# A hybrid decoder layer on one core: the first projection fed by k tiles, some waits re-ordered, and two early transfers issued by ScalarE

## The chip, the cores and the metric

The kernel runs on one core of a Trainium2 chip. The metric is the device time of one execution in microseconds (us). A core has five instruction streams that matter here: TensorE (PE in the profile; PEld are its weight loads), VectorE (DVE), ScalarE (ACT), GpSimd (POOL) and SyncE (SP), which only issues transfers. ACT can issue transfers too; ACTq and SPq are the rows for that.

## The reference

One layer over x of 256 tokens by 2048 channels, all in float32:

```python
h = rmsnorm(x, norm_mix_pre)
xr, yr, q, k, v, g_rnn, g_attn = split(h @ w_in)
y_rnn = rg_lru(conv(xr)) * gelu(yr)
y_att = sliding_window_sink_attention(rope(q), rope(k), v, sinks)   # 32 query heads, 4 key/value heads of 64
mix = sigmoid(g_rnn) * (y_rnn @ w_rnn_proj) + sigmoid(g_attn) * (y_att @ w_attn_proj)
x = x + rmsnorm(mix @ w_out, norm_mix_post)
u = square(relu(rmsnorm(x, norm_mlp_pre) @ w_mlp_up))               # 8192 wide
x = x + rmsnorm(u @ w_mlp_down, norm_mlp_post)
```

## The kernel before, in words

**Products.** Each float32 operand is split into a rounded part "hi" and a remainder "lo"; a product is three matmuls, hi·hi, hi·lo and lo·hi. `Stream` (L56 to L170) feeds the weights: a half chunk of 128 x 1024 floats (512 KB) is loaded into `wraw`, ACT casts it into `whi` (L107, L116), DVE subtracts to get `wlo` (L108, L124). There are four `wraw` buffers and six each of `whi` and `wlo`; `ahead` (L151) keeps the split six halves in front of PE.

**The opening (L342 to L470).** k and v of all 256 tokens are one product over 16 k tiles of 128 channels, accumulated in two banks `kv`, one for each block of 128 tokens. The weights `w_kv` come as eight halves of two k tiles each; x transposed (`x_t`) comes as five further transfers; the gains lie in the table `tiny`, which ACT loads (L350) while SP issues all else. `part(k)` (L400) multiplies a tile of x by its gain on ACT and makes the remainder on DVE: `hT`. `split_first` (L66) splits the first half in two pieces, `kv_step` (L408) issues the matmuls (L415), 12 for each half and pass over tokens; ten matmuls on a tile of ones (`warm`, L396) run in front. Loads of the next weights (`w_g`) and of x itself (`xq`, for the norm) follow on SP.

**The passes that follow.** Gates and queries (`b_pass512`), then the recurrent branch (`a_pair`, L256). Attention is a generator for each of four head groups; `pump` advances the oldest generator by one step at four places in each `a_pair` and at one in each step of `b_pass512`, so its instructions lie between the matmuls of the projection. `turn_probs` (L625) transposes the probabilities on PE into banks `pt`, which ACT copies out (L638).

**The norm between mix and MLP (L950 to L1040).** The last matmuls of `w_out`, the norm of the second token block (`norm(1)`), its transposes (`turned`, L973, into two banks used in turn) and the first matmuls of the MLP (`up_step`, L1027) are interlaced by hand. `high` (L978, ACT) and `low` (L983, DVE) empty a bank.

**The end (L1142 to L1285).** `down` sums 16 pairs of k tiles into four output blocks (token block, column block); seven of the pairs are combined in seven products in place of eight (`SEVEN`, the last is pair 12), and their sums are added into tiles `ready` (L1175 to L1179) and to the running sum `acc` (L1243). Pair 13 goes to all four blocks, then for each block in turn come the matmuls of pairs 14 and 15 and `finish` (L1260): add the bank (L1269), square with a running sum on ACT (L1270), multiply by the gain (L1271); after a token block's last column block follow sum, square root, reciprocal (L1275 to L1277), the scaled addition (L1283) and the store (L1284).

**Order.** Each engine runs its instructions in order. What `pin` wraps keeps the order of the program; the rest is ordered by the framework's planner, which gives earlier lines priority among those that are ready by its own reckoning.

Of the kernel before, what the change touches and what calls it, by code (L numbers as in the profile page):

```python
# [53 lines left out]
class Stream:  # L54
# [3 lines left out]
    def __init__(self, nc, pool, chunks, room, sums):  # L58
        self.nc, self.pool, self.chunks, self.room, self.sums = nc, pool, chunks, room, sums
        self.raw, self.parts = {}, {}  # L60
        self.loaded = self.split = 0
        self.pin = lambda i: i
        self.high = []
        self.at = 0

    def split_first(self, between):  # L66

        src = self.raw.pop(0)
        hi = self.pool.tile([P, 1024], F32R, tag="whi", bufs=WHALF, name="whi0")
        lo = self.pool.tile([P, 1024], F32R, tag="wlo", bufs=WHALF, name="wlo0")  # L70
        for i in range(2):
            c = slice(i * 512, i * 512 + 512)
            self.pin(self.nc.scalar.copy(hi[:, c], src[:, c]))
            between(i)
            self.pin(self.nc.vector.tensor_tensor(lo[:, c], src[:, c], hi[:, c].bitcast(F32), ALU.subtract))
        self.parts[0] = hi, lo
        self.split = 1

    def load_to(self, n):
        while self.loaded < min(n, 2 * len(self.chunks)):  # L80
            j = self.loaded
            c = slice(j % 2 * 1024, j % 2 * 1024 + 1024)
            if j < 2 * EXTRA:
                if j % 2 == 0:
                    self.place = self.room(f"wraw{j}")
                t = self.place[:, c]
            else:
                t = self.pool.tile([P, 1024], F32, tag="wraw", bufs=WRAW, name=f"wraw{j}")
            self.latest = self.nc.sync.dma_start(t, self.chunks[j // 2][:, c])
            self.raw[j] = t  # L90
            self.loaded += 1
# [85 lines left out]
EXTRA = 5  # L177


def layer(tc, x, x_t, few, pos_row, gains, w_kv, w_q, w_xy, w_rg, w_g, w_rp, w_ap, w_out,  # L180
# [13 lines left out]
    chunks = [w_kv[i] for i in range(4)]  # L194
# [145 lines left out]
    xts = [flat(unit(f"xt{i}", F32)) for i in range(2)]  # L340

    def xt(k, n=1):  # L342
        return xts[k // 8][:, k % 8 * S : (k % 8 + n) * S]

# [4 lines left out]
    tiny = const.tile([P, 210], F32, name="tiny")  # L349
    nc.scalar.dma_start(tiny, few)  # L350
    gcol, ifr, sink = [tiny[:, a : a + n] for a, n in ((0, KT), (16, 32), (48, NH))]
    vec = tiny[:, 80:208].rearrange("p (a b) -> p a b", a=8)
    pos_i = tiny[:, 208:210].bitcast(I32)

    def load_xt(a, b):
        q, c = a // 4, slice(a % 4 * S, a % 4 * S + (b - a) * S)
        nc.sync.dma_start(xt(a, b - a), x_t[q][:, c])
# [13 lines left out]
    ws.load_to(2 * EXTRA + WRAW)  # L371
# [6 lines left out]
    sq = const.tile([P, 4, TB, 4], F32, name="sqs")  # L378
# [21 lines left out]
    def part(k):  # L400
        q, i, g, src = k // 4, k % 4, gcol[:, k : k + 1], xt(k)
# [6 lines left out]
    def kv_step(j):  # L408
        hi, lo = ws.half(False)
        for ks in ((0,), (1,)) if j == 0 else ((0, 1),):  # L410
            for x, w in ((0, hi), (1, hi), (0, lo)):
                for tb in range(TB):
                    for i in ks:
                        kt = 2 * j + i
                        pin(mm(kv[tb], hT[kt // 4][:, kt % 4, x, tb * P : tb * P + P], w[:, quarter(i)],  # L415
                               start=kt == 0 and w is hi and x == 0, stop=kt == KT - 1 and w is lo))
# [40 lines left out]
    ws.split_first(part)  # L457
    kv_step(0)
    angle = angles()
    for j in range(1, 8):  # L460
        for i in range(2):
            part(2 * j + i)
        ws.split_high()
        ws.split_low()
        kv_step(j)
        if j > 3:
# [84 lines left out]
    def attention(g, banks):  # L551
# [73 lines left out]
        def turn_probs(tb, pars=(0, 1)):  # L625
# [5 lines left out]
            for par in pars:  # L631
                for kb in range(nk):
                    ps = bank(psm, "pt")
# [37 lines left out]
        yield  # L671
        turn_probs(1, (1,))
        yield
        for tb in range(TB):
# [280 lines left out]
    def norm(tb, between=None, late=None):  # L955
# [4 lines left out]
        if between:  # L960
            between()
        pin(nc.vector.reciprocal(a, b))
        for q in range(4):
            c = quarter(q)
            if q == 3 and late:
                late()
            pin(nc.vector.scalar_tensor_tensor(h2[tb][:, c], h2[tb][:, c], a, xg[tb][:, c], ALU.mult, ALU.add))
        r1.append(a)

# [47 lines left out]
    norm(1, lambda: low(0, 3), lambda: gained(1, 3, banks[1][1]))  # L1017
    for j in range(3):
# [12 lines left out]
    for q, n in enumerate((26, 6, 6, 6)):  # L1031
# [4 lines left out]
        high(1, q)  # L1036
        low(1, q)
        if q == 1:
# [92 lines left out]
    def product(b, a, w, begun, tail=False):  # L1131

        for i, (x, y) in enumerate(((0, 0), (0, 1), (1, 0))):
            mm(b, a[x], w[y], start=not begun and i == 0, stop=tail and i == 2)  # L1134
# [7 lines left out]
    def down(f, n, uT, held, order, finish, early, between=lambda p: None, behind=lambda: None):  # L1142
# [8 lines left out]
        def step(p, parts, names):  # L1151
            for name in names:
                at, n2 = name
                b = PLACE[name]
                for i, (hi, lo) in enumerate(parts):
                    t = slice(at * P, at * P + P)
                    c = quarter(n2)
                    a = uT[p][:, i]
                    product(banks[b], (a[:, 0, t], a[:, 1, t]), (hi[:, c], lo[:, c]), b in begun,
                            p == PAIRS - 1 and i == 1)  # L1160
                    begun.add(b)

        ready = {}
        for p in range(PAIRS - held):
            if p in SEVEN:
                parts = ws.seven()
                for name, (i, w) in LEFT.items():
                    product(banks[name], (uT[p][:, 0, i], uT[p][:, 1, i]), parts[w], name in begun,
                            p == SEVEN[-1] and name in ("P1", "P6", "Q5", "N7"))
# [11 lines left out]
            else:  # L1181
                for i in range(2):
                    hi, lo = ws.half()
                    for name in order:
                        at, n2 = name
                        b = PLACE[name]
                        t, c = slice(at * P, at * P + P), quarter(n2)
                        a = uT[p][:, i]
                        product(banks[b], (a[:, 0, t], a[:, 1, t]), (hi[:, c], lo[:, c]), b in begun)
                        begun.add(b)  # L1190
            between(p)
        parts = [[ws.half(False) for i in range(2)] for p in range(held)]
        behind()
        for name in order:
            for i in range(held):
                step(PAIRS - held + i, parts[i], (name,))
            finish(name, banks[PLACE[name]], ready[name])
        ws.ahead(ws.at - 1)

    for f in range(2):  # L1200
# [25 lines left out]
        if f == 0:  # L1226
            for n in range(2):
                def finish(name, b, t):
# [31 lines left out]
        def finish(name, b, t):  # L1260
# [4 lines left out]
            if n == 0:  # L1265
                nc.vector.tensor_tensor(a, b, t, ALU.add)
                nc.scalar.activation(t, a, AF.Square, accum_out=sq[:, 3, tb, q : q + 1])
                return
            pin(nc.vector.tensor_tensor(a, b, t, ALU.add))  # L1269
            pin(nc.scalar.activation(spare[:, c], a, AF.Square, accum_out=sq[:, 3, tb, q : q + 1]))  # L1270
# [100 lines left out]
```

## Time and profile before

| | us |
|---|---|
| median of 3 runs (1502.19 to 1502.8) | 1502.19 |
| the profiled execution's own time | 1502.42 |
| its span, first to last instruction | 1500.6 |
| PE busy | 1485.3 |
| DVE busy | 1097.8 |
| ACT busy | 829.6 |

The profile is one execution taken by the hardware profiler. The span is 1.8 us shorter than the execution's time; the rest lies around it. A busy PE says that matmuls were in flight, not that they ran at full clock, so the granted clock is read beside it. A row of the timeline gives start, duration, engine, line of the code, operation, what is written and read, shapes, and in brackets how long the engine had idled before and what released it.

### The profile page before, as it was taken

To read this page: it belongs to the slowest core of one execution; us is meant where nothing else is said; L and a number is where in the kernel's file an instruction comes from. 1 tells how busy PE (TensorE), PEld (TensorE's weight loads), DVE (VectorE), ACT (ScalarE), POOL (GpSimd) and SP (SyncE) were. 2 spreads that over 40 slices of the span, in tenths; PEclk is the share of its full clock that TensorE was granted. 3 is DMA by queue.
4 is the path that set the end of the run, shared out by engine and by line. 5 is a ranking of instruction groups with operands and counts; after the bars stand their busy time and mean duration, and the time that the engine had idled before them with its cause. 6 is when DMAs were issued, how large, how long until landed. Compare 5 with 4: busy or idle time off the path is not lost.

```text
span 1500.6 us, 19926 instructions
## 1 busy us (share of the span) xinstructions
PE 1485.3 (99%) x7568; PEld 1259.0 (84%) x7568; DVE 1097.8 (73%) x1356; ACT 829.6 (55%) x1137; POOL 1.7 (0%) x9
## 2 busy tenths in 40 slices
PE   9999999999999999999999999999999999999997
PEld 7887788788889888888889888888888888888886
DVE  6576668859669966555658866798886666788897
ACT  7564665647567665444355654555454555455453
POOL 0000000000000000000000000000000000000000
PEclk9999999999999999999999999999999999999999
DMA  8654554565646556555764765566667555566665
GB/s 339 217 161 156 166 163 136 169 195 172 210 155 211 179 200 208 184 191 188 276 216 144 262 190 192 186 208 206 210 204 242 189 193 187 192 239 210 204 215 186
DMA packets 83471, 298.28 MB, mean 199 GB/s; under 512 B 9264, under 2 KB 9520, under 8 KB 82352
## 3 DMA queue, kind: packets, MB, share of 16 engines
q1 hardware_dynamic: 80064, 289.57, 58.2%
q10 hardware_dynamic: 3312, 7.45, 1.4%
q8 instruction: 59, 0.97, 0.3%
q14 instruction: 36, 0.29, 0.1%
HBM read 290.69 MB, written 6.29 MB: 198 GB/s over the span
## 4 chain that ended last, share of the span: by engine, by line
PE 97%; DVE 2%; DMA 0%; ACT 0%; issue 0%; DVEq 0%; SPq 0%; ACTq 0%
PE ps L269 22%; PE ps L267 12%; PE dQ L1134 9%; PE s L1134 5%; PE dP L1134 4%; PE g L307 4%; PE g L311 4%; PE g L309 4%; PE pp L309 4%; PE pp L307 4%; PE pp L311 4%; PE dCs L1134 3%; PE q L307 2%; PE q L311 2%; PE q L309 2%; PE o L307 2%
## 5 line engine op out<-in xcount | busy, mean ns | idle before, releaser
L108 DVE TENSOR_TENSOR wlo<-wraw,whi 128x1024 fp32r<-128x1024 f32 x516 | 625.2, 1222 | 309.0 <-ACT whi L107 305.8
L107 ACT CAST whi<-wraw 128x1024 fp32r<-128x1024 f32 x516 | 537.8, 1051 | 546.5 <-PE ps L269 129.7
L269 PE MATMUL ps<-h2T,whi 128*128 128x512 f32 x960 | 223.9, 390 | 0.0
L269 PEld LDWEIGHTS ps<-h2T,whi 128*128 128x128 f32 x960 | 178.2, 188 | 35.7
L267 PEld LDWEIGHTS ps<-h2T,wlo 128*128 128x128 f32 x960 | 119.1, 192 | 2.3
L269 PE MATMUL ps<-hT,whi 128*128 128x512 f32 x512 | 120.7, 391 | 0.0
L267 PE MATMUL ps<-h2T,wlo 128*128 128x256 f32 x960 | 119.9, 283 | 0.0
L269 PEld LDWEIGHTS ps<-hT,whi 128*128 128x128 f32 x512 | 94.8, 188 | 20.3 <-issue 1.5
L1134 PE MATMUL dQ<-whi,uT 128*128 128x512 f32 x288 | 106.8, 389 | 0.0
L307 PE MATMUL g<-whi,hT 128*128 128x512 f32 x256 | 101.1, 395 | 0.0
L311 PE MATMUL g<-whi,hT 128*128 128x512 f32 x256 | 99.8, 390 | 0.0
L309 PE MATMUL g<-wlo,hT 128*128 128x512 f32 x256 | 99.8, 390 | 0.0
L267 PEld LDWEIGHTS ps<-hT,wlo 128*128 128x128 f32 x512 | 63.7, 192 | 1.2
L267 PE MATMUL ps<-hT,wlo 128*128 128x256 f32 x512 | 64.4, 283 | 0.0
L1134 PEld LDWEIGHTS dQ<-whi,uT 128*128 128x128 f32 x288 | 54.1, 188 | 11.2
L307 PEld LDWEIGHTS g<-whi,hT 128*128 128x128 f32 x256 | 48.1, 188 | 10.6 <-issue 1.0
L311 PEld LDWEIGHTS g<-whi,hT 128*128 128x128 f32 x256 | 48.0, 188 | 10.2
L309 PEld LDWEIGHTS g<-wlo,hT 128*128 128x128 f32 x256 | 48.1, 188 | 9.6
L1134 PE MATMUL dQ<-wlo,uT 128*128 128x512 f32 x144 | 56.0, 389 | 0.0
L1134 PE MATMUL dP<-whi,uT 128*128 128x512 f32 x144 | 54.1, 389 | 0.0
L1134 PE MATMUL dCs<-whi,uT 128*128 128x512 f32 x144 | 54.1, 389 | 0.0
L143 DVE TENSOR_TENSOR tlo<-t,thi 128x1536 fp32r<-128x1536 f32 x28 | 49.2, 1757 | 6.4 <-ACT thi L142 5.9
(284 smaller groups left out, 2464.5 us busy)
## 6 DMA issues: line engine op xcount, KB each, us to landing
wraw<-in_w_up SPq DMA_DIRECT2D x128, 512.0 KB, 4.1
wraw<-in_w_dn SPq DMA_DIRECT2D x128, 512.0 KB, 4.6
wraw<-in_w_g SPq DMA_DIRECT2D x64, 512.0 KB, 4.6
wraw<-in_w_xy SPq DMA_DIRECT2D x64, 512.0 KB, 4.6
wraw<-in_w_q SPq DMA_DIRECT2D x32, 512.0 KB, 4.4
wraw<-in_w_ap SPq DMA_DIRECT2D x32, 512.0 KB, 4.5
wraw<-in_w_rp SPq DMA_DIRECT2D x32, 512.0 KB, 3.8
wraw<-in_w_out SPq DMA_DIRECT2D x32, 512.0 KB, 5.1
```

Of the source, the lines that this page charges most:

```text
L107: self.pin(self.nc.scalar.copy(hi, src))
L108: self.pin(self.nc.vector.tensor_tensor(lo, src, hi.bitcast(F32), ALU.subtract))
L143: v.tensor_tensor(lo, t, hi.bitcast(F32), ALU.subtract)
L267: mm(ps[:, f, 1, :], w, a[:, 0, :], start=False, stop=j == 1 and k == 7)
L269: mm(ps[:, f].rearrange("p a b -> p (a b)"), w, a.rearrange("p a b -> p (a b)"), start=kt == 0, stop=j == 3 and k == 7)
L307: mm(banks[tb][n], a[:, 0, t], hi[:, n * 512 : n * 512 + 512], start=first, stop=False)
L309: mm(banks[tb][n], a[:, 0, t], lo[:, n * 512 : n * 512 + 512], start=False, stop=False)
L311: mm(banks[tb][n], a[:, 1, t], hi[:, n * 512 : n * 512 + 512], start=False, stop=last)
L1134: mm(b, a[x], w[y], start=not begun and i == 0, stop=tail and i == 2)
```

## The change

- **Opening.** The host lays weights and transposed x of one k tile side by side: `kx_first` (768 columns and the 16 gains, 392 KB) and 15 tiles `kx_rest` (768 columns, 384 KB). One transfer brings all that a k tile needs. Tiles 1 and 3 are issued on ACT's queue, all others on SP's; the table `tiny` without the gains comes on SP behind tile 5. `kv_step` works by k tile: the weights' cast of 512 columns (tile 0 on DVE, the others on ACT), `part`, the remainder, six matmuls. The stream of halves begins with `w_g`, with four halves loaded in front instead of six.
- **Attention of the last group.** The scores of the last heads and their masking fall in one step, both transposing steps of the second token block in one, the second into banks of the other pool, and one empty step is added before the output product. All from the masking on comes one pump earlier, the second transposing step two.
- **The norm.** Of the three casts of MLP weights in front of the transposes one is moved behind the first bank's `high`; the fourth quarter's gain and scaling are moved behind the first bank's `low`.
- **The end.** Pair 13 is put to blocks (0,0) and (0,1) only; blocks (1,0) and (1,1) get it together with pairs 14 and 15. Block (1,1) is done in two halves of 256 columns, the second in a fresh bank; what its old bank holds there is added earlier (`fold`). All four stores of the first token block follow block (0,1).

```diff
@@ Stream
-        self.loaded = self.split = 0
+        self.loaded = self.split = self.at = FIRST
...
-        self.load_to(max(2 * EXTRA, j + WHALF) + WRAW)
+        self.load_to(max(FIRST, j + WHALF) + WRAW)
...
+FIRST = 8
...
-    chunks = [w_kv[i] for i in range(4)]
+    chunks = [None] * (FIRST // 2)
@@ layer, loads
-    tiny = const.tile([P, 210], F32, name="tiny")
-    nc.scalar.dma_start(tiny, few)
...
-    ws.load_to(1)
-    load_xt(0, 2)
-    load_xt(2, 4)
-    ws.load_to(2)
-    for q in range(1, 4):
-        load_xt(4 * q, 4 * q + 4)
-        ws.load_to(2 * q + 2)
-    ws.load_to(12)
+    tiny = const.tile([P, 194], F32, name="tiny")
...
+    kx, at = [], 0
+    for k in range(KT):
+        if k % 2 == 0:
+            place, at = flat(unit(f"kx{k}", F32)), 0
+        n = 512 + S + (KT if k == 0 else 0)
+        kx.append(place[:, at : at + n])
+        at += n
+        (nc.scalar if k in (1, 3) else nc.sync).dma_start(kx[k], kx_rest[k - 1] if k else kx_first)
+        if k == 5:
+            nc.sync.dma_start(tiny, few)
+    gcol = kx[0][:, 512 + S :]
+    ws.load_to(FIRST + WRAW)
...
-    ws.load_to(2 * EXTRA + WRAW)
@@ layer, k and v
-    def kv_step(j):
-        hi, lo = ws.half(False)
-        for ks in ((0,), (1,)) if j == 0 else ((0, 1),):
...
+    def kv_step(kt, hi, lo):
+        c, src = quarter(kt % 2), kx[kt][:, 0:512]
+        if kt:
+            pin(nc.scalar.copy(hi[:, c], src))
+        else:
+            pin(nc.vector.tensor_copy(hi[:, c], src))
+        part(kt)
+        pin(nc.vector.tensor_tensor(lo[:, c], src, hi[:, c].bitcast(F32), ALU.subtract))
+        for x, w in ((0, hi), (1, hi), (0, lo)):
+            for tb in range(TB):
+                pin(mm(kv[tb], hT[kt // 4][:, kt % 4, x, tb * P : tb * P + P], w[:, c],
+                       start=kt == 0 and w is hi and x == 0, stop=kt == KT - 1 and w is lo))
@@ attention
-                    ps = bank(psm, "pt")
+                    ps = bank(psb if last_group and tb and par else psm, "pt")
...
             three = scores(1, 1, [bank(psb, "sc") for par in range(2)])
-            yield
         masked(*three)
...
         turn_probs(1, (0,))
-        yield
+        if not last_group:
+            yield
         turn_probs(1, (1,))
         yield
+        if last_group:
+            yield
@@ norm
-    norm(1, lambda: low(0, 3), lambda: gained(1, 3, banks[1][1]))
-    for j in range(3):
+    norm(1, lambda: low(0, 3))
+    for j in range(2):
         begun.append(ws.split_high())
...
         high(1, q)
+        if q == 0:
+            begun.append(ws.split_high())
         low(1, q)
+        if q == 0:
+            gained(1, 3, banks[1][1])
+            scaled(1, 3)
@@ down
-        for p in range(PAIRS - held):
+        for p in range(PAIRS - held - closing):
...
+        if closing:
+            for i in range(2):
+                parts.append((PAIRS - held - 1, i) + ws.half())
+                for name in order[:2]:
+                    step(*parts[i], name)
...
+            if closing and k == 1:
+                a, r = order[-1], slice(256, 512)
+                fold = lambda: pin(v.tensor_tensor(ready[a][:, r], banks[PLACE[a]][:, r], ready[a][:, r], ALU.add))
+                for e in todo:
+                    step(*e, name)
+                finish(name, b, t, 0, 512, fold)
+            elif closing and k == 3:
+                for e in todo:
+                    step(*e, name, 0, 256)
+                finish(name, b, t, 0, 256)
+                for e in todo:
+                    step(*e, name, 256, 256, "P1")
+                finish(name, banks["P1"], t, 256, 256)
@@ finish
-            for tb, qs in {(0, 1): ((0, (2, 0)),), (1, 0): ((0, (1, 3)),), (1, 1): ((1, (2, 0, 1, 3)),)}.get(name, ()):
+            for tb, qs in {(0, 1): ((0, (2, 0, 1, 3)),), (1, 1): ((1, (2, 0, 1, 3)),)}.get(name, ()):
```

More of the change, by code (lines that the diff above doesn't have):

```diff
@@ L455, in sines @@
             nc.vector.tensor_scalar(ss[:, :, i, :], sn, 1.0 - 2.0 * i, None, ALU.mult)
-    ws.split_first(part)
-    kv_step(0)
     angle = angles()
[L460 to L466, printed above, removed]
+    for kt in range(KT):
+        if kt % 2 == 0:
+            halves = [wpool.tile([P, 1024], F32R, tag=tag, bufs=WHALF, name=f"{tag}{kt // 2}") for tag in ("whi", "wlo")]
+        kv_step(kt, *halves)
+        if kt > 8 and kt % 2:
             next(angle, None)
@@ L959, in norm @@
         pin(nc.scalar.activation(b, a, AF.Sqrt, bias=eps, scale=1.0 / D))
-        if between:
-            between()
+        between()
         pin(nc.vector.reciprocal(a, b))
[L963 to L967, printed above, removed]
         r1.append(a)
+        for q in range(4 - tb):
+            scaled(tb, q)
     def turned(tb, q):
@@ L1140, in layer, with down @@
     PLACE = {(0, 0): "Q4", (0, 1): "Cs", (1, 0): "P2", (1, 1): "Q3"}
-    def down(f, n, uT, held, order, finish, early, between=lambda p: None, behind=lambda: None):
+    def down(f, n, uT, held, order, finish, early, between=lambda p: None, behind=lambda: None, closing=False):
         two = [pair(f"s{i}") for i in range(2)]
@@ L1291, in layer @@
         g3 = flat(unit("g3", F32))
-        down(f, n, uT, 2, [(0, 0), (0, 1), (1, 0), (1, 1)], finish, early, between, behind)
+        down(f, n, uT, 2, [(0, 0), (0, 1), (1, 0), (1, 1)], finish, early, between, behind, True)
     ctx2.close()
```

127 lines of the change are left out of this document (54 added, 73 removed).

## The prediction, made before the change was run

> **What bounds the kernel now.** I read the page first, then the waits of PE, then the chain of work that ended last.
>
> ```profile
> PE 1485.3 (99%) x7568; PEld 1259.0 (84%) x7568; DVE 1097.8 (73%) x1356; ACT 829.6 (55%) x1137; POOL 1.7 (0%) x9
> ```
>
> ```profile
> PE kv L415 <- ACT hT L402: 2.5, 1, 2.5
> PE pt L636 <- ACT pT L638: 1.4, 1, 1.4
> PE ptr L973 <- DVE h2T L983: 0.7, 1, 0.7
> ```
>
> ```profile
> 7.43 23.63 PE kv L415 x96
> ```
>
> ```profile
> 1300.56 7.28 PE ps L269 x32
> 1307.84 3.83 PE ps L267 x32
> ```
>
> PE works for 1485.3 us, 99% of the span of 1500.6 in the table; 15.3 us are left. These waits make 4.6 of them; the rest lies before PE's first work and at the end, where it has nothing more to do. So the change, which removes no matmul, can win in four places alone: how soon `kv` begins, the wait at `pt`, the wait at `ptr`, and the end. A matmul of 512 columns (L269) costs 7.28 / 32 = 0.227 us, one of 256 columns (L267) 3.83 / 32 = 0.12. At that price the 96 of `kv` take 21.8 us, and they take 23.63: something slows them. The granted clock (last column but two) tells what.
>
> ```profile
> 7.00:7.50 0.50, 0.07 (x1) 0.07 (x1) 0.09 (x1) 0.50 (x2) 0.00 (x0) 0.86 1.01 406
> 7.50:8.00 0.50, 0.50 (x1) 0.43 (x2) 0.50 (x2) 0.50 (x2) 0.00 (x0) 0.50 1.00 410
> ```
>
> ```profile
> 10.50:11.00 0.50, 0.50 (x3) 0.38 (x2) 0.50 (x1) 0.36 (x1) 0.00 (x0) 0.73 1.02 418
> ```
>
> It falls to half at 7.36 (0.86 is full speed for 0.36 of 0.5 us) and comes back at 10.77: 3.41 us at half speed, 1.7 us lost.
>
> **The opening: start of kv, -0.5 us.**
>
> ```profile
> 0.74 0.38 SPq L89 DMA_DIRECT2D wraw<-in_w_kv  x1
> ```
>
> ```profile
> 6.16 0.62 ACT L73 CAST whi<-wraw 128x512 fp32r<-128x512 f32 x1 [3.49 <-DMA wraw<-in_w_kv]
> 6.87 0.51 ACT L402 ACTIVATE hT<-xt,tiny 128x256 fp32r<-128x256 f32 x1
> ```
>
> ```profile
> 7.81 0.68 DVE L75 TENSOR_TENSOR wlo<-wraw,whi 128x512 fp32r<-128x512 f32 x1
> ```
>
> ```profile
> 1.17 5.61 DMA xt<-in_x_t
> ```
>
> Before, ACT casts when the weights land (6.16), multiplies when x has landed too (6.78), and PE starts at 7.43, 0.56 after that instruction begins. After, one transfer brings both, and the cast of tile 0 on DVE lies beside ACT's multiplication. The trace has no DVE copy of this size; its price lies between nothing and the 0.68 of the subtraction, and I take 0.68, the nearest row. So PE starts 0.7 us after tile 0 lands. When is that? The table that ACT issued in before ran beside the first weights:
>
> ```profile
> q1 hardware_dynamic: 20, 0.08, 45.3%
> q10 hardware_dynamic: 19, 0.02, 38.2%
> ```
>
> These are the two queues' packets from 3.0 to 3.5 us (packets, MB, share of the engines): 20 and 19, turn by turn, at nearly the same engine time though one kind is 4 KB and the other under 1 KB. In the first microseconds a packet costs time, not bytes. The first weights are 128 rows, tile 0 is 128 rows; the table was 128 rows, tile 1 is 128 rows. I therefore let tile 0 land when the first weights did, 6.2, and PE start at 6.9: 0.5 us sooner. Bounds: tiles 0 and 1 have 794 KB together, as much as the weights and the first x (786 KB), which had landed at 6.78; then PE starts at 7.5, +0.1. If tile 0 goes as fast as a median weight load in mid-kernel,
>
> ```profile
> wraw<-in_w_up SPq DMA_DIRECT2D x128, 512.0 KB, 4.1
> ```
>
> it lands at 4.8 and PE starts at 5.5: -1.9.
>
> The Trainium skill, "DMA: Bandwidth & Descriptors", section "Issuing engines are not separate DMA queues", says that transfers from different engines run on the same 16 DMA engines and interleave, and that issuing from several saves only issue time. That speaks against the ACT queue here: issue takes 0.38 us a transfer, and tile 1 would share tile 0's time. The interleaved packets above agree; by the opposite rule the start would be near the lower bound.
>
> Once kv runs, each k tile needs 1.36 us of PE at full clock. ACT has 0.62 + 0.51, DVE 0.68 and about half a microsecond for the smaller remainder, less than PE. A tile's 393 KB at the 410 GB/s of the clock rows (last column) take 0.96. ACT's two issues lie in its idle time ahead of 6.16. So nothing but the start moves, and the table behind tile 5 is needed only from the tenth tile on. The two halves of `w_g` no longer loaded in front wait for their buffers, but PE needs the first of these 10 us later than it could be split. I cost both at nothing; without that cover each would cost a load of 4 us.
>
> **The opening: the clock, 0 us.**
>
> ```profile
> 1.08 3.85 PE L396 MATMUL warm<-ones 128*128 128x128 f32 x20 [1.08 <-DVE ones L380]
> ```
>
> The clock fell at the end of a stretch in which PE worked on the tile of ones until 4.93 and then stood. If the gate looks back over the 3.41 us that the slow stretch lasts, it saw 0.98 us of work (29%) between 3.95 and 7.36. With a start at 6.9 it would see 1.44 (42%). Nothing here shows where the line lies, so I leave the slow stretch in and make its absence a rival.
>
> **Attention, -1.4 us.**
>
> ```profile
> 277.78 1.03 PE L636 MATMUL pt<-ident,s 128*128 128x128 f32 x8
> ```
>
> ```profile
> 281.51 1.14 PE L636 MATMUL pt<-ident,s 128*128 128x128 f32 x8 [1.39 <-ACT pT L638]
> ```
>
> ```profile
> 274.35 2.49 DVE L620 TENSOR_TENSOR s<-s,stat 128x512 f32<-128x512 f32 x4
> ```
>
> The second eight transposes wait for the banks of the first, which ACT empties late. With two banks of another pool all sixteen run together, one pump sooner than the first eight did, and the output product comes two pumps behind, time for four copies on ACT. The wait goes: 1.4. What may be late next are the shares on DVE (L620), which end at 276.84, when the transposes are to begin at about 274 (a pump, 16 matmuls of 0.227, before 277.78). They are issued one pump earlier as well, some 4 us, so I expect them in time. If they stay where they are, PE waits 2.8 instead of 1.4: +1.4.
>
> **The norm, -0.4 us.**
>
> ```profile
> 806.97 0.75 DVE L967 SCALAR_TENSOR_TENSOR h<-h,st,xg 128x512 f32<-128x512 f32 x1
> 807.63 1.28 DVE L983 TENSOR_TENSOR h2T<-ptr,h2T 128x512 fp32r<-128x512 f32 x2
> ```
>
> ```profile
> 808.37 0.66 PE L973 MATMUL ptr<-ident,h 128*128 128x128 f32 x4 [0.70 <-DVE h2T L983]
> ```
>
> ```profile
> 809.58 0.60 PE L973 MATMUL ptr<-ident,h 128*128 128x128 f32 x4
> ```
>
> PE stands from 807.67 to 808.37 for the bank that L983 empties. After, L983 precedes gain and scaling (0.6 + 0.7 us) and ends at about 807.1: no wait. But the two moved instructions now precede the second L983, which ends at 807.1 + 0.6 + 0.7 + 0.7 = 809.1, and PE is at the last transposes at 808.8. They start near 809.2 instead of 809.58: 0.4 won of 0.7. Bounds: -0.7, and +0.6 if the moved cast (1 us) comes to stand ahead of a `high`.
>
> **The end, +0.2 us.**
>
> ```profile
> 1478.68 1.23 DVE L108 TENSOR_TENSOR wlo<-wraw,whi 128x1024 fp32r<-128x1024 f32 x1 [0.25 <-ACT whi L107]
> ...
> 1484.02 0.69 DVE L1269 TENSOR_TENSOR acc<-dQ,t 128x512 f32<-128x512 f32 x1
> 1484.74 0.69 DVE L1271 TENSOR_TENSOR t<-acc,g 128x512 f32<-128x512 f32 x1
> ...
> 1491.76 0.68 DVE L1269 TENSOR_TENSOR acc<-dQ,t 128x512 f32<-128x512 f32 x1
> ...
> 1493.29 0.16 DVE L1275 TENSOR_REDUCE st<-sqs 128x1 f32<-128x4 f32 x1
> ...
> 1494.01 0.75 DVE L1283 SCALAR_TENSOR_TENSOR x<-t,st,x 128x512 f32<-128x512 f32 x1
> ```
>
> ```profile
> 1495.42 1.32 DVE x L1283 x2
> ```
>
> ```profile
> 1490.58 0.39 PE L1134 MATMUL dQ<-whi,uT 128*128 128x512 f32 x1
> ```
>
> ```profile
> L518 DVE TENSOR_TENSOR qr<-ra,rb x8: 421/424/428, 76.9 to 240.3; 128x256 f32<-128x256 f32 x8
> ```
>
> PE is done at 1490.97, yet the last bank is added at 1491.76: DVE is behind: from the last `wlo` at 1478.68 on it adds up `ready` and `acc`, and it begins `finish` of (0,0) at 1484.02, when PE had done that bank three blocks of 12 matmuls before its end, at 1482.8. After, PE does it 2.7 us sooner (only half of pair 13 comes before), but nothing that DVE does ahead of it is removed. So I start DVE at 1484.02 again and add its steps: 0.72 from L1269 to L1271 and some 0.6 to the next block; 0.35 for the fold; 0.7 from the sum L1275 to the first scaled addition (1493.29 to 1494.01); four of these at 0.66. Block (1,0) begins at 1490.4, the first half of (1,1) at 1491.7, the second at 1492.5 (a 256-column instruction has 0.42). PE, with 18 matmuls at 0.12 twice in place of 18 at 0.227 (+0.2) and some 0.3 waited for the last `wlo`, which ends at 1479.9 and is now wanted at 1479.6, is done at 1491.6, ahead of DVE. Square and running sum of 256 columns are 0.2 shorter, so the sum L1275 comes at 1493.5 against 1493.29: +0.2, and all behind it is as before. Bounds: -0.8 if DVE reaches (0,0) early enough that PE sets the end, 1.1 us behind 1491.6; +1.0 if the planner puts other work between.
>
> **The sum** is -0.5 + 0 - 1.4 - 0.4 + 0.2 = -2.1 us. The profiled execution took 1502.42, 0.2 over the median 1502.19, which is less than most terms; applied to the median, 1500.1.
>
> **Rivals.**
>
> *The clock is spared* (chance 0.28). PE starts so soon that the gate sees enough work: 1.7 us more, 1498.4. For it: at the end PE works to 1490.97, and the clock falls only at 1495.6 (0.79 in the row), not at the turn 3.41 us before, which had seen 65% of work.
>
> ```profile
> 1495.00:1496.00 1.00, 0.00 (x0) 0.00 (x0) 1.00 (x2) 0.00 (x0) 0.00 (x0) 0.79 0.37 145
> ```
>
> So the line lies between 29% and 65%, and 42% falls in between. The Trainium skill, "TensorE: Matmul & The Clock Gate", section "Part 1: The HAM clock gate (the "warmup" mystery)", lets the clock fall after an idle window of about 3.4 us. Taken at its word no window here would be idle, and this rival would be certain; but the clock fell in before after a window with 29% of work, so the measurement decides against that reading.
>
> *The second queue adds speed* (0.10). Tile 0 lands at 4.8, PE starts at 5.5, the gate sees 0.98 + 1.86 us, 83%, and the clock stays: -1.9 - 1.7 - 1.4 - 0.4 + 0.2 = -5.2, 1497.0. Against it stand the interleaved packets.
>
> *The transposes wait for the shares* (0.14). In attention DVE keeps its order and PE, with sixteen transposes in one step, waits 2.8 us: -0.5 + 1.4 - 0.4 + 0.2 = +0.7, 1502.9, slower than before. It decides from the point where L620 ends 1.4 us behind PE's arrival. With every other upper bound (+0.1, +0.6, +1.0) it reaches +3.1.
>
> **How the numbers follow.** My forecast has 0.48. What this kernel's measurement can tell from no change is about 0.2%, 3.0 us, so faster means under 1499.2. That holds for nine in ten of the spared clock (0.25), the second queue (0.10) and 0.15 of the forecast's own case (0.07): 0.42. Slower by as much needs nearly all upper bounds: 0.06. The rest, 0.52, is no change that can be told. The range goes from 1497.0 to 1502.7; it holds the first two cases and cuts the other two.
>
> **What would show it.** The first `kv` matmul at 6.9; packets of both queues turn by turn; the clock at half from about 7.4 for 3.4 us; no wait of PE at `pt`, and L620 done before the transposes; about 0.4 us of wait at the last `ptr`; DVE without a gap up to the last L1269 at the end. Wrong would be a start before 6 or after 7.5, a full clock throughout, a wait at `pt` of over 1 us, or a PE that ends later than DVE's turn to add.

## The result, and the profile after

The changed kernel takes 1495.99 us (median of 4 runs, 1495.84 to 1496.03) against 1502.49 (4 runs, 1502.19 to 1503.18): a ratio of 0.9957, 95% interval [0.9945, 0.9969], 6.5 us less. The forecast was 2.1 us less. The profiled execution took 1495.84 with a span of 1493.9. One of the 11 runs of same_places, below, took 2499 us; it enters no ratio.

The page's busy times of the changed kernel, and then all that its view of PE's waits lists (engine and line <- releaser: us in total, times, longest):

```profile
PE 1484.6 (99%) x7586; PEld 1259.3 (84%) x7586; DVE 1097.6 (73%) x1367; ACT 829.8 (56%) x1145; POOL 1.7 (0%) x9
```

```profile
PE warm L370 <- DVE ones L354: 1.1, 1, 1.1
PE kv L392 <- ACT hT L376: 0.4, 1, 0.4
PE pt L609 <- DVE s L593: 0.2, 1, 0.2
```

Of the waits of 2.5, 1.4 and 0.7 us, 0.4 and 0.2 are left, and the one at `ptr` is gone. The opening, in the timeline of the changed kernel:

```profile
5.14 0.43 DVE L387 CAST whi<-kx 128x512 fp32r<-128x512 f32 x1 [4.11 <-DMA kx<-in_kx_first]
5.14 0.51 ACT L376 ACTIVATE hT<-kx 128x256 fp32r<-128x256 f32 x1 [1.99 <-DMA kx<-in_kx_first]
5.56 0.60 ACT L385 CAST whi<-kx 128x512 fp32r<-128x512 f32 x1
...
5.71 1.24 PE L392 MATMUL kv<-whi,hT 128*128 128x512 f32 x4 [0.39 <-ACT hT L376]
```

Tile 0 lands at 5.14, not at 6.2, and ACT casts tile 1 at 5.56 without having waited for it: both tiles, 794 KB, are there 1.2 us before the first 786 KB were in the kernel before. The windows of the changed kernel (busy times of five engines, then the granted clock, the share of the DMA engines, GB/s):

```profile
3.00:3.50 0.50, 0.50 (x4) 0.50 (x4) 0.00 (x0) 0.15 (x1) 0.00 (x0) 1.00 0.92 329
3.50:4.00 0.50, 0.50 (x4) 0.50 (x4) 0.00 (x0) 0.00 (x0) 0.00 (x0) 1.00 1.04 422
...
7.50:8.00 0.50, 0.50 (x4) 0.41 (x3) 0.27 (x1) 0.50 (x3) 0.00 (x0) 1.00 1.03 399
```

The transfers reach 422 GB/s before 4 us; in the kernel before those two windows moved 196 and 243. The clock stays full: the first four `kv` matmuls take 1.24 us, and in the kernel before they took 2.07:

```profile
7.43 2.07 PE L415 MATMUL kv<-whi,hT 128*128 128x512 f32 x4 [2.50 <-ACT hT L402]
```

And the loads are faster not only here. The page's rows of transfers (count, KB each, median us from issue to landing), where the kernel before has 4.1 and 4.6; the medians of the other six weight tensors are lower too, by 0.1 to 0.8 us:

```profile
wraw<-in_w_up SPq DMA_DIRECT2D x128, 512.0 KB, 3.7
wraw<-in_w_dn SPq DMA_DIRECT2D x128, 512.0 KB, 4.1
```

These transfers are issued by the same code from inputs that the diff does not touch. That is what the prediction had not seen, and most experiments go after it.

In attention the transposes now come up against the shares (L593), as one rival had it, but for 0.2 us:

```profile
271.27 0.38 PE L609 MATMUL pt<-ident,s 128*128 128x128 f32 x2
...
271.89 1.75 PE L609 MATMUL pt<-ident,s 128*128 128x128 f32 x14 [0.24 <-DVE s L593]
```

In the norm PE no longer stands, and ten `ps` matmuls instead of six lie between the last two transposing steps, so four more are done when the last begins:

```profile
802.34 0.69 DVE L958 TENSOR_TENSOR h2T<-ptr,h2T 128x512 fp32r<-128x512 f32 x1
...
803.39 0.60 PE L948 MATMUL ptr<-ident,h 128*128 128x128 f32 x4
...
803.74 1.43 PE L1002 MATMUL ps<-h2T,whi 128*128 128x256 f32 x10
...
805.08 0.65 PE L948 MATMUL ptr<-ident,h 128*128 128x128 f32 x4
```

At the end DVE begins to add up the banks (L1269) long before PE is done, and now waits for PE:

```profile
1470.37 1.23 DVE L89 TENSOR_TENSOR wlo<-wraw,whi 128x1024 fp32r<-128x1024 f32 x1 [1.06 <-ACT whi L88]
...
1475.71 0.68 DVE L1269 TENSOR_TENSOR acc<-dQ,t 128x512 f32<-128x512 f32 x1
...
1486.30 0.42 DVE L1269 TENSOR_TENSOR acc<-s,t 128x256 f32<-128x256 f32 x1 [1.16 <-PE s L1114]
```

```profile
1485.98 0.28 PE L1114 MATMUL s<-whi,uT 128*128 128x256 f32 x1
```

PE ends at 1486.26. The last `wlo` begins 15.9 us ahead of that (before: 1490.97 - 1478.68 = 12.3), DVE's first L1269 10.6 ahead (before: 6.95), and 7.6 us follow PE's end (before: 9.6).

### The profile page after: what moved, and what is told of

It is laid out like the page before. It is cut to its first block, busy times and chain, and to the rows that moved or that the text cites. A ratio compares the mean times of both kernels' runs of the same rounds, so it can differ in the third digit from the quotient of the medians.

```text
span 1493.9 us, 19993 instructions
## 1 busy us (share of the span) xinstructions
PE 1484.6 (99%) x7586; PEld 1259.3 (84%) x7586; DVE 1097.6 (73%) x1367; ACT 829.8 (56%) x1145; POOL 1.7 (0%) x9
## 4 chain that ended last, share of the span: by engine, by line
PE 97%; DVE 1%; ACT 1%; DMA 0%; issue 0%; DVEq 0%; ACTq 0%
PE ps L250 21%; PE ps L248 11%; PE dQ L1114 9%; PE s L1114 5%; PE dP L1114 5%; PE g L288 4%; PE g L292 4%; PE g L290 4%; PE pp L292 4%; PE pp L290 4%; PE pp L288 4%; PE dCs L1114 3%; PE q L288 2%; PE q L292 2%; PE q L290 2%; PE o L288 2%
## 5 line engine op out<-in xcount | busy, mean ns | idle before, releaser
L1114 PE MATMUL dQ<-whi,uT 128*128 128x512 f32 (+1 forms) x288 | 105.3, 385 | 0.0
L288 PEld LDWEIGHTS g<-whi,hT 128*128 128x128 f32 x256 | 48.1, 188 | 10.6 <-issue 1.0
L1114 PE MATMUL dQ<-wlo,uT 128*128 128x512 f32 (+1 forms) x144 | 55.4, 385 | 0.0
```

Of the source, the lines that this page charges most:

```text
L288: mm(banks[tb][n], a[:, 0, t], hi[:, n * 512 : n * 512 + 512], start=first, stop=False)
```

## The experiments

The theory at this point: the parts gain what the milestones below say, and a third of the gain is none of theirs, since all loads are faster. Rivals for the loads: ScalarE's queue, the small packets of the table, the place of the buffers in SBUF, the order of work, the place of the inputs in DRAM. Each ratio is to the kernel before on the same chip. The milestones (us, profiled executions): first `g` matmul, first `pp` on `yatt` (behind the attention), last transposes `ptr`, end of PE, span.

| kernel | g | pp | ptr | PE's end | span |
|---|---|---|---|---|---|
| before | 30.90 | 291.59 | 809.58 | 1490.97 | 1500.6 |
| changed | 27.85 | 287.52 | 805.08 | 1486.26 | 1493.9 |
| waits_only | 30.75 | 290.56 | 808.13 | 1489.30 | 1499.0 |
| open_only | 27.87 | 288.57 | 806.54 | 1487.92 | 1496.8 |
| all_but_end | 27.78 | 287.58 | 805.28 | 1486.25 | 1495.1 |
| inputs_last | 27.95 | 287.63 | 805.21 | 1488.38 | 1496.6 |
| same_places | 30.44 | 291.11 | 809.08 | 1490.46 | 1499.4 |

### The queue and the table

**sp_only**, on the changed kernel:

```diff
-        (nc.scalar if k in (1, 3) else nc.sync).dma_start(...)
+        nc.sync.dma_start(...)
```

> The changed kernel with tiles 1 and 3 issued by SyncE like the others. Theory A (small packets): in the kernel before, the first weights were slow because the table's 128 short rows ran beside them; the second queue adds no speed and takes half the packets. Then tile 0, alone in front, lands sooner than the 5.14 us of the changed kernel, at 4.4 to 5.0, the first kv matmul comes at 5.0 to 5.6 (5.71 changed), tile 1 lands at 5.5 to 6 and may be waited for; time 1495.3 to 1496.3. Theory B (the second queue adds speed): tile 0 lands later, 5.7 to 6.2, PE starts at 6.3 to 6.8; time 1496.6 to 1497.2, and 1498 to 1499 if the clock then falls to half.

Measured: 1496.67 us, ratio 0.9958 [0.9946, 0.9971]. In its timeline tile 0 lands and PE starts at:

```profile
3.93 0.43 DVE L387 CAST whi<-kx 128x512 fp32r<-128x512 f32 x1 [2.90 <-DMA kx<-in_kx_first]
...
4.70 1.27 PE L392 MATMUL kv<-whi,hT 128*128 128x512 f32 x4
```

So ScalarE's queue speeds nothing: it makes tile 0 land 1.2 us later, as tile 1 shares its time, and the first `g` comes at 27.07 without it, 0.8 us sooner. In the whole time that can't be told from the changed kernel.

**table_first**: the same, and the table goes first, on ScalarE's queue, as in the kernel before.

> The changed kernel with all tiles on SyncE and the table of 194 columns issued by ScalarE first, as the kernel before had it. Theory A (small packets): tile 0 lands near 6.1 as the first weights did, PE starts near 6.7, 1 us later than in the changed kernel; with the clock spared 1497.0, with the slow stretch 1498.7. Theory B (the second queue adds speed, whatever it carries): tile 0 lands at 5.1 as in the changed kernel, time 1496.0.

Measured: 1496.01 us, 0.9954 [0.994, 0.9968]; tile 0 lands at 4.33, PE starts at 5.37. The table costs tile 0 0.4 us, and its small packets are not what slowed the old opening.

### The clock

**warm_long**, on the kernel before:

```diff
-WARM = 10
+WARM = 15
```

> The kernel before with 15 matmuls on the tile of ones instead of 10, so that PE stands at most 0.5 us before kv. Clock theory: the granted clock stays full, kv takes about 21.9 us instead of 23.6; time 1500.5 to 1501.0 (1.7 less than before, less what the longer row of ones delays kv). Rival (kv is slow for another reason, data or splits): kv stays at 23.5, time 1502.2 to 1503.

Measured: 1501.39 us, 0.9986 [0.9978, 0.9995], 2.1 us less by the ratio. `kv` starts at 7.31, and its first four matmuls take 1.25 us instead of 2.07. From there to the first `g` 22.2 us pass instead of 23.5: of the 1.7 us that the prediction read from the slow stretch, 1.3 come through.

### The parts

**waits_only**: the kernel before with the changes of attention and norm alone. **open_only**: with the opening alone.

> The kernel before with the re-ordered attention and norm alone; opening and end are the old ones. If the stretch between the first gate matmul and the MLP lost 4.9 - 3.0 = 1.9 us through these two edits (1.1 attention, 0.8 norm), this kernel is 1.9 us faster than before, its waits at pt and ptr are under 0.3 us, and its landing times are those of before. If half of it came from faster loads, it gains 1 us or less.

> The kernel before with the new opening alone; attention, norm and end are the old ones, and its weight buffers lie at multiples of 64 as in before. The opening was worth 3.0 us at the first gate matmul (30.90 to 27.90). If the place in SBUF makes the loads fast, this kernel loads as before does (w_up 4.2, w_dn 4.7), tile 0 lands at 5.7 to 6.2 and it gains 2 to 2.5 us. If the inputs' layout in DRAM does it, w_up lands in 3.7, w_dn in 4.1, tile 0 at 5.1, and it gains 3 us from the opening and up to 1 more at the old end, where the last split waited 2.74 us for its transfer: 3 to 4.

Measured: waits_only 1500.97 us, 0.9986 [0.9977, 0.9994]; open_only 1499.03, 0.9973 [0.9962, 0.9983]. In waits_only attention is worth 0.9 us (1.03 less the 0.15 of its start), the norm up to PE's end 0.6 more; the loads are as before (w_up 4.3, w_dn 4.7). In open_only the first `g` is 3.0 us sooner and the loads are fast (3.8, 4.2), with the weight buffers at the addresses of the kernel before; the old end gives 0.8 more.

**end_only**: the new end alone on the kernel before.

> The kernel before with the new end alone. Theory C (the order does it): PE ends 0.2 us later and the rest behind it shrinks from 9.6 to 7.6 us, time 1500.4 to 1500.9. Theory D (the prediction's working: VectorE is behind when it reaches block (0,0), as in the profile before): time 1502.4 to 1502.9. What tells them apart within the profile is when VectorE begins the first addition of block (0,0), counted from PE's last matmul: 7.0 us before PE's end is D, over 9 us before it is C.

Measured: 1503.97 us, 1.0004 [0.9995, 1.0013]: nothing. Its view of PE's waits has two rows at the end that the changed kernel does not have:

```profile
PE dQ L1135 <- DVE wlo L108: 1.4, 2, 0.8
...
PE dQ L1135 <- ACT whi L107: 0.9, 1, 0.9
```

PE wants pair 13 sooner and finds it not split, because it is loaded late (w_dn 4.8; in the changed kernel, with 4.1, the same order has no such wait). DVE begins block (0,0) 7.8 us ahead of PE's end, between the two marks that were set.

**all_but_end** (the changed kernel with the old end) and **after_again** (the changed kernel), on one chip:

> The changed kernel with the old end; opening, attention and norm are the new ones. With the old opening the new end alone gained nothing. If the faster loads let DVE keep up with PE so that the new order of the end pays, this kernel is 1 to 2 us over the changed kernel of the same call. If the new end is worth nothing in itself (the +0.2 of the forecast) and all the gain at the end comes from the loads, it is within 0.5 us of the changed kernel.

> The changed kernel itself, for comparison on the same chip with the runs of this call: 1495.8 to 1497, ratio to the kernel before 0.9945 to 0.9969; w_up 3.7, w_dn 4.1.

Measured: 1497.28 us, 0.9965 [0.9953, 0.9978], and 1496.31, 0.9961 [0.9948, 0.9973]. The medians are 1.0 us apart (runs of 1497.0 to 1498.2 and of 1496.1 to 1497.4), though the ratios' intervals overlap; the profiles say the same: behind PE's end follow 1495.1 - 1486.25 = 8.85 us with the old end and 7.64 with the new one, which has 0.2 us more of matmuls. In the timeline of all_but_end, whose L1249 is the L1269 of the changed kernel:

```profile
1478.16 0.68 DVE L1249 TENSOR_TENSOR acc<-dQ,t 128x512 f32<-128x512 f32 x1
```

That is 8.1 us ahead of PE's end, against 6.95 with slow loads: DVE, too, is fed by the loads.

### What makes the loads fast

**The place in SBUF.** In the first runs the weight buffers of the fast kernels lay 32 bytes above a multiple of 64. **pad_before** and **pad_after** are the two kernels with an unused tile ahead of all others:

```diff
+    pad = const.tile([P, 8], F32, name="pad")
+    nc.vector.memset(pad, 0.0)
```

> The kernel before with one unused constant tile of 32 bytes a partition ahead of all others (and the memset that fills it), so that every later tile lies 32 bytes further on in SBUF; nothing else differs. In all runs so far the kernels with the new opening have their weight buffers at addresses that are 32 above a multiple of 64 and load faster in mid-kernel (the page's median landing of w_up 3.7 us, w_dn 4.1 to 4.2, against 4.1 to 4.5 and 4.6 to 4.8 with the old opening, at multiples of 64). If the place in SBUF makes the loads fast: w_up 3.7, w_dn 4.2, rate of the first transfers (2.5 to 4.0 us) near 360 GB/s in place of 280, x and first weights landing some 0.5 us earlier, time 0.3 to 1.5 us under the kernel before. If the inputs' layout in DRAM (or the order of the inputs) makes them fast: w_up 4.2 to 4.5, w_dn 4.6 to 4.8, about 280 GB/s, and the time of the kernel before within 1 us.

> The changed kernel with the same unused tile of 32 bytes, so that its weight buffers come back to multiples of 64; nothing else differs. If the place in SBUF makes the loads fast, this one is slow to load: w_up 4.2, w_dn 4.7, tile 0 of the opening some 0.5 to 1 us later (5.7 to 6.2), DVE late again at the end, time 1497.5 to 1499. If the inputs' layout in DRAM does it: w_up 3.7, w_dn 4.1, tile 0 at 5.1, time 1495.8 to 1497, that of the changed kernel.

Measured: pad_before 1502.69 us, 0.9994 [0.9985, 1.0003], w_up 4.1, w_dn 4.7; pad_after 1496.26, 0.9955 [0.9942, 0.9967], 3.8 and 4.2. The place in SBUF is out.

**Inputs against order of work.** **inputs_moved** is the kernel before with another order of its inputs, **new_inputs** its order of work on the new inputs, **old_inputs** the new order of work on the old inputs, **inputs_last** the changed kernel with two inputs declared elsewhere:

```diff
-def layer(tc, x, few, kx_first, kx_rest, pos_row, ... w_up, w_dn, out):
+def layer(tc, x, few, pos_row, ... w_up, w_dn, kx_first, kx_rest, out):
```

> The kernel before, instruction for instruction; only the order in which its inputs are declared is another: x, few, x_t, w_kv, pos_row, gains, w_q and so on, in place of x, x_t, few, pos_row, gains, w_kv, w_q: the order in which the changed kernel has its own. If where the inputs lie in DRAM by their order makes the loads fast: w_up 3.7, w_dn 4.1 to 4.2, and up to 1 us less time through earlier last splits. If order is nothing (sizes of the inputs, or the new opening's instructions): w_up 4.1 to 4.5, w_dn 4.6 to 4.8, time of the kernel before.

> The kernel before with its old order of work, but weights and transposed x read from the new inputs kx_first and kx_rest, in pieces of 2 KB (weights) and 1 KB (x); the first half of the weights and the first x come in two transfers each. If the new inputs make the loads of mid-kernel fast: w_up 3.7, w_dn 4.1 to 4.2, though the opening itself, with twice the packets, comes 0.5 to 2 us later. If the order of work of the new opening does it (which buffers are loaded first, how many halves lie in front): w_up 4.1 to 4.5, w_dn 4.6 to 4.8.

> The changed kernel in all its order of work, but each k tile is read from the old inputs w_kv and x_t in two transfers, and the table with the gains comes first on ScalarE's queue; all tiles on SyncE's queue. If the inputs make the loads fast, this one loads slowly: w_up 4.1 to 4.5, w_dn 4.6 to 4.8; time 1497.5 to 1500. If the order of work does it: w_up 3.7, w_dn 4.1, time 1496 to 1497.5.

> The changed kernel, instruction for instruction, with kx_first and kx_rest declared last, behind w_dn, so that every other input has another place. If the place decides, the loads are slow (w_up 4.1 to 4.5, w_dn 4.6 to 4.8) or at least other than in the changed kernel, and tile 0 lands later than 5.1; time 1497 to 1499. If only what the opening reads matters: w_up 3.7, w_dn 4.1, tile 0 at 5.1, time 1495.8 to 1496.7.

| kernel | us | ratio | w_up | w_dn |
|---|---|---|---|---|
| inputs_moved | 1502.53 | 0.9999 [0.999, 1.0008] | 4.0 | 4.7 |
| new_inputs | 1500.11 | 0.9987 [0.9977, 0.9997] | 3.7 | 4.3 |
| old_inputs | 1501.94 | 0.9996 [0.9985, 1.0006] | 3.9 | 4.7 |
| inputs_last | 1498.47 | 0.9975 [0.9964, 0.9986] | 4.0 | 4.7 |

The old order of work loads fast from the new inputs, the new order loads slowly from the old ones. And inputs_last, which runs the changed kernel's instructions, loads the weights as the kernel before does. Its row for `w_dn`, and the waits of its PE at the end:

```profile
wraw<-in_w_dn SPq DMA_DIRECT2D x128, 512.0 KB, 4.7
```

```profile
PE dQ L1114 <- DVE wlo L89: 0.8, 1, 0.8
```

Up to the last `ptr` it keeps step with the changed kernel (805.21 and 805.08); then it loses 2.0 us up to PE's end and 0.6 behind it (8.22 against 7.64). Of the 2.0, 0.8 are this wait and 0.3 one at `ps`; the rest no row of the waits names.

Its opening stays fast all the same: 373 and 416 GB/s where the changed kernel has 329 and 422. So the ramp of the first microseconds is a matter of its own. The windows of old_inputs, then those of table_first, which issues its tiles in the same order with the table first:

```profile
3.00:3.50 0.50, 0.50 (x4) 0.50 (x4) 0.00 (x0) 0.00 (x0) 0.00 (x0) 1.00 0.60 198
3.50:4.00 0.50, 0.50 (x4) 0.50 (x4) 0.00 (x0) 0.00 (x0) 0.00 (x0) 1.00 1.07 191
```

```profile
3.00:3.50 0.50, 0.50 (x4) 0.50 (x4) 0.00 (x0) 0.00 (x0) 0.00 (x0) 1.00 1.08 391
3.50:4.00 0.50, 0.50 (x4) 0.50 (x4) 0.00 (x0) 0.00 (x0) 0.00 (x0) 1.00 1.07 398
```

The tensor that is read sets the ramp: here half the rate from `w_kv` and `x_t`. It is not the size of the pieces: new_inputs reads the new tensors in pieces of 2 and 1 KB, as old_inputs reads the old ones, and has 374 and 352 GB/s. Over all profiles the nine that read `w_kv` and `x_t` have 195 to 282 GB/s from 3 to 4 us, the eleven that read the new tensors 357 to 395. The place by order of declaration did not change it: inputs_last is fast, inputs_moved (249) and same_places below (239) are slow. The price of old_inputs is not to be taken as that of the loads alone: its 32 transfers of the opening stand ahead of `w_g` on SyncE's queue, PE waits 2.25 us for a remainder of `w_g` at 39.7, and the granted clock is 0.50 from 40 to 43 us.

**How small a step?** **spare_before** and **spare_after** have one unused input of 1 KB more, behind x.

> The kernel before, instruction for instruction, with one more input of 1 KB declared behind x and used by nothing, so that every later input is laid a little further on in DRAM, if inputs are laid one behind the other in the order of their declaration. If the place alone decides, and a small step of it: w_up 3.7, w_dn 4.1 to 4.3 in place of 4.1 and 4.6, and 0.5 to 2.5 us less time. If the place decides, but not by so small a step, or if it is the inputs' sizes or shapes: w_up 4.0 to 4.3, w_dn 4.6 to 4.8, and the time of the kernel before within 1 us.

> The changed kernel, instruction for instruction, with the same unused input of 1 KB behind x. If a small step of the place decides, the loads turn slow (w_up 4.0, w_dn 4.7) and the time is that of the run with the inputs of the opening declared last: 2 to 3 us over the changed kernel. If not: w_up 3.7, w_dn 4.1, and the changed kernel's time within 0.7 us.

Measured: 1502.97 us, 1.0001 [0.9992, 1.001], w_up 4.4, w_dn 4.6; and 1496.52, 0.996 [0.9947, 0.9974], 3.8 and 4.3. A small step does nothing.

**The place alone.** **same_places** is the kernel before, its inputs in the order

```diff
-def layer(tc, x, x_t, few, pos_row, gains, w_kv, w_q, ... w_up, w_dn, out):
+def layer(tc, x, few, spare_a, spare_b, pos_row, gains, w_q, ... w_up, w_dn, x_t, w_kv, out):
```

with two unused inputs of the shapes of `kx_first` and `kx_rest`. **first_last** is the changed kernel with `kx_first` alone declared last.

> The kernel before, instruction for instruction; two unused inputs of the shapes of kx_first and kx_rest are declared where the changed kernel has those, and x_t and w_kv come last, so that every other input is declared behind the same sizes as in the changed kernel. If the place of the weights alone makes the loads fast: w_up 3.7 to 3.8, w_dn 4.1 to 4.3, and 1 to 2.6 us less time than before, the loss at the end of the run with the inputs declared last given back. If something else of the changed kernel must be there as well: w_up 4.0 to 4.4, w_dn 4.6 to 4.8, and the time of the kernel before within 1 us.

> The changed kernel with kx_first alone declared last; kx_rest keeps its place ahead of the weights. If kx_rest, 5.9 MB and no power of two, is what shifts the weights: w_up 3.7, w_dn 4.1 to 4.3 and the changed kernel's time within 0.7 us. If the 392 KB of kx_first do it: w_up 4.0, w_dn 4.7 and 2 to 3 us more.

Measured: same_places 1501.08 us, 0.9986 [0.9976, 0.9995], 2.1 us less by the ratio; first_last 1496.08, 0.9956 [0.9942, 0.9969], with 3.7 and 4.3. The rows of same_places:

```profile
wraw<-in_w_up SPq DMA_DIRECT2D x128, 512.0 KB, 3.8
wraw<-in_w_dn SPq DMA_DIRECT2D x128, 512.0 KB, 4.2
```

No instruction is other than before, and the loads are those of the changed kernel. So what is declared ahead of the weights makes them fast, and of the two new inputs `kx_rest`, 5.9 MB, is enough. That `x_t` and `w_kv` are gone from ahead of them is not it: inputs_last has neither of the two, and is slow. In the profile 0.5 us of it come at the start and 0.7 behind PE's end.

## Why the prediction was wrong

The direction was right, and so were attention and norm in the main; the size was three times too small, and the time lies 1.0 us below the range. Point by point, in us:

| step | forecast | profile | kernels that show it |
|---|---|---|---|
| start of `kv` | -0.5 | -1.7 | old_inputs, table_first, sp_only |
| clock | 0 | -1.3 | warm_long |
| attention | -1.4 | -1.0 | waits_only |
| norm | -0.4 | -0.8 | waits_only |
| end | +0.2 | -1.8 | all_but_end, same_places |

**The start: the step that failed** is "In the first microseconds a packet costs time, not bytes", and with it "I therefore let tile 0 land when the first weights did, 6.2"; it landed at 5.14. The reading rested on half a microsecond of one execution, 45.3 and 38.2% of the engines for 20 and 19 packets. In the seven other profiles with the old opening (warm_long among them) the 4 KB packets of that half microsecond took 52 to 95%, and about as many short ones 13 to 23%: bytes cost time. So a tile of half the bytes lands sooner, also from the old inputs: in old_inputs the 393 KB of tile 0 are there at 5.36, where 786 KB were needed and there at 6.78 before, and PE starts at 5.92. That is 1.5 of the 1.7 us. The new inputs, with their faster ramp and one transfer in place of two, land tile 0 another 1.0 us sooner (4.33 in table_first), of which PE, still at work on the tile of ones, uses 0.5; ScalarE's queue takes 0.3 of that back (5.71).

The turns of the two queues were right (26 and 27 packets from 3.0 to 3.5), and so was the rule of the Trainium skill, "DMA: Bandwidth & Descriptors", "Issuing engines are not separate DMA queues", that they interleave. The table, to which the reading gave half the time, costs 0.4. The rival "the second queue adds speed" has nearly the right start (5.5 against 5.71), but by luck: without that queue the start is 4.70.

**The clock** followed from the start. With `kv` at 5.71 PE stood 0.39 us and ran at full pace: 1.3 us saved, as in warm_long; 0.4 of the 1.7 go to small waits between PE and the splits of the first tiles. Where the line lies, for which the prediction found no row, stays open. In the seven profiles with the old opening and ten matmuls on the tile of ones, PE stood 1.32, 1.75, 2.04, 2.26, 2.30 and 2.50 us and a stretch of half pace came in `kv`; it stood 1.79 (end_only) and none came:

```profile
7.51 1.25 PE L416 MATMUL kv<-whi,hT 128*128 128x512 f32 x4 [1.79 <-ACT hT L403]
```

So the length of the gap alone does not decide. The two shortest gaps can't be read from the granted clock. In same_places it is 1.00, but PE's row has the 2.08 us of half pace, and from `kv` to the first `g` 23.4 us pass (23.5 before, 22.1 in end_only):

```profile
7.50:8.00 0.50, 0.50 (x2) 0.36 (x2) 0.50 (x1) 0.50 (x2) 0.00 (x0) 1.00 1.04 410
```

```profile
7.03 2.08 PE L415 MATMUL kv<-whi,hT 128*128 128x512 f32 x4 [1.32 <-ACT hT L402]
```

The forecast's own start, 6.9 less 4.93, is a gap of 1.97, between the 1.79 and the 2.04, so these rows do not fault its 0 for that start. "The clock is spared" named what happened, PE beginning soon enough; its 1498.4 counted 0.4 too much for the pace and lacked the rest of the start and the faster loads.

**Attention** was right but for 0.4: 0.2 of it is the new wait for the shares, the rest no row names. **The norm** was under-sized: the prediction held PE up at the last transposes for the two moved instructions, and they do begin 0.4 sooner, as forecast (4.50 - 4.07 from `pp` to `ptr`), but PE does four more matmuls (4 x 0.12) ahead of them, so that about the whole wait of 0.7 is won. (From `pp` to PE's end the changed kernel gains 4.71 - 4.07 = 0.64, in spite of the 0.2 that the end adds: 0.8 in the table; waits_only has 0.6.)

**The end: the second step that failed** is "So I start DVE at 1484.02 again", for "nothing that DVE does ahead of it is removed". What DVE does was not removed, but it comes sooner, as the loads feed it: 8.1 us ahead of PE's end instead of 6.95 with the old end (all_but_end, same_places: 8.85 and 8.94 us behind PE's end instead of 9.63). With DVE in time the new end pays: 8.85 to 7.64, less 0.2 for the smaller matmuls. On slow loads it pays nothing (end_only); there PE waits for splits, as the prediction's 0.3 for the last `wlo` had it, only more (2.3).

The sum of the profile, -3.0 for the opening, -1.0, -0.8 and -1.8, is -6.6 of the 6.7 us in span. How much is due to what is declared ahead of the weights alone: 2.1 us in the kernel before (same_places), some 2.1 in the changed kernel (0.9975 for inputs_last, 0.9961 for after_again, on two chips), both with intervals of over 1 us to each side. No row of the trace before tells of it; a range that took such an effect in would have had to come from doubt that a change of input layout is neutral for all else.

## What to carry to other kernels

A change of an input's layout is two changes: what the kernel does with it, and where all inputs behind it lie. Before a gain is put down to the code, compare the landing times of transfers that the change does not touch; if they moved, run the old code with unused inputs in the new one's places. And where one engine splits and adds what another multiplies, the worth of a re-ordered end depends on how early its loads land: the same edit was worth nothing and about 1 us here.

## What the runs showed of the hardware

- **What is declared ahead.** Loads of 512 KB landed in 3.7 to 3.8 us (w_up) and 4.1 to 4.3 (w_dn) in all kernels with 5.9 MB of `kx_rest`, or an unused input of its shape, declared ahead of the weights, and in 3.9 to 4.5 and 4.6 to 4.8 in all others; two pairs have the same instructions (before and same_places, changed and inputs_last). Order of equal inputs, 1 KB more, and 32 bytes in SBUF changed nothing. That the place in DRAM is what changes is an inference, and which property of the addresses does it is open: the trace shows no addresses in DRAM. The Trainium skill, "DMA: Bandwidth & Descriptors", section "Latency and other measured facts", tells of slow copies where rows lie 512 KiB or more apart at a power of two, and calls the mechanism an inference; the rows here lie 8 KB apart in fast and slow kernels alike, so the case is not covered by it.
- **The ramp of the first transfers** depends on the tensor that is read: 191 to 198 GB/s between 3 and 4 us from `w_kv` and `x_t`, 391 to 398 from the new tiles, in the same order of issue. It stayed when either was declared elsewhere, which speaks for the layout; no run changed the layout alone.
- **A second queue** delayed what was wanted first by 1.2 us (5.14 against 3.93), and added nothing to the rate (329 and 422 GB/s from 3 to 4 us, 380 and 393 without it).
- **The granted clock** of the profile's first microseconds can read 1.00 while PE runs at half pace: in same_places and pad_before four `kv` matmuls took 2.08 and 2.07 us at 1.00, in the kernel before 2.07 at 0.50, in end_only 1.25 at 1.00. The pace of the matmuls is the surer sign there.
